# Moving the first five parts of a head's scan later in the product stream of the next head (HGRN2, odd heads)

## The chip, the cores and the metric

The kernel runs on one core of a Trainium2 chip. The metric is the device time of one execution in microseconds (us), as the median of several runs. The engines are TensorE (PE in the profile; its weight loads are PEld), VectorE (DVE), ScalarE (ACT), GpSimd (POOL) and SyncE (SP, which issues most of the transfers). Each engine works through its own instructions in the order in which they were written, and waits on the others through semaphores.

## The reference, cut to what matters

One step of a two-layer decoder over 512 prompt tokens and 64 sample tokens (8 sequences of 8), width 1024, all in float32. Layer 0 mixes tokens with HGRN2, a gated linear recurrence with 8 heads of width 128; layer 1 uses an S5 state-space model. The change touches layer 0's mixer alone:

```python
q, fz, v, g = jnp.split(x @ w_in, 4, axis=-1)
f = lbf + (1.0 - lbf) * sigmoid(fz)
qh = heads(silu(q) * HG_QK_SCALE); kh = heads(1.0 - f)
# per head: S_t = diag(f_t) S_{t-1} + k_t v_t^T,  o_t = S_t^T q_t
o, s = hgrn2_chunk_scan(qh, kh, heads(v), heads(log(f)), s0)
o = rms_norm(o, gnorm_w) * silu(heads(g))
return o @ w_out, s
```

The prompt starts from a zero state, the sample sequences from given states; the new states of both are outputs.

## The kernel before, in words

**Products.** A float32 product is made of three matmuls of split operands (`mm3`, lines 299 to 301: high by high, high by low, low by high). "A product" below means one such triple, over one of the 8 slices of the width. The projections of a head are written by the generator `proj(h)`, which gives back control after every product. The weights of f, q and g take 16 products each: 8 for the first 320 tokens, into one PSUM bank, and 8 for the other 256, into a second one. So an odd head has 48 products, numbered 0 to 47 (0 to 7 with 320 columns, 8 to 15 with 256, and so on). An even head first has 40 products more, the value projection V for itself and the head after it.

**What is written between the products.** After each product the loop at the end of `hgrn()` writes one step of the oldest of the `sides` (`decay`, `factors`, `queries`: the elementwise work of a head on ACT, DVE and POOL), and then the steps of `scan(h-1)`, the recurrence of the head before, that the table `SCAN_AT` lists for this number. `SCAN_AT[0]` is for even heads and `SCAN_AT[1]` for odd ones. Head 0 has no scan to carry, so the odd row serves four heads, 1, 3, 5 and 7, with the scans of heads 0, 2, 4 and 6. Nothing else sets the order: what is written first stands first in its engine's queue.

**The sides around the place.** `factors(h-1)` runs in the last third of `proj(h-1)` and ends with the decayed keys K2 and the factors QL and E2. `queries(h-1)` counts nine empty steps (`QWAIT`) and so acts at products 9 to 12 of the next head: at 9, ACT copies both PSUM banks of g, loads the Silu table, applies Silu to a 128 by 1152 tile and loads the log/exp table again; at 10 to 12, DVE writes QH, the three pieces of QL, and Q2.

**The scan's 16 steps.** Step 1 transposes K2 on PE (line 661), copies the result into kT on ACT and has POOL mask the values into vm. Step 2 transposes the sample part (line 668) and copies it. Step 3 multiplies kT by V (line 674), copies the first of four states to S on ACT and adds up the other three on DVE, and has SP send the last one out. Step 4 makes the sample state updates on PE (line 688, one bank from the ring `tr`, one from the ring `mm`), and DVE adds the first four of them to So; step 5 adds the other four. Steps 6 to 9 are the attention blocks within a chunk of 128 tokens (lines 704 and 709: KH by QH, and KL by QL); step 6 also has SP send So out. Steps 10 to 16 make the outputs.

**Banks.** The ring `tr` has two banks, taken in turn by steps 1, 2, 3, 4 (its first bank) and 6. So step 6 takes the bank that step 3 had, and its first matmul may run only when ACT and DVE have read that bank; step 3 takes the bank of step 1, and step 4 that of step 2. The ring `mm` of four banks serves the products and step 4. In the trace, names lose their last digits: K is K2, Q is Q2, S and So are as written, and many DVE and ACT operations carry the line of a helper (L200, L203, L206, L197).

Of the kernel before, what the change touches and what calls it, by code (L numbers as in the profile page):

```python
# [62 lines left out]
SY = ((6, 8), (8, 8), (6, 10), (6, 2))  # L63
QY = ((3, 3), (2, 5), (1, 3), (1, 2))
SPLIT_S5 = 14
SCAN_AT = ((2, 4, 10, 16, 20, 26, 30, 34, 38, 42, 46, 50, 54, 60, 68, 74), (2, 4, 6, 9, 12, 15, 17, 19, 21, 23, 26, 33, 34, 36, 41, 45))
QWAIT = 9
SIDE = 1
OCT = 2
# [73 lines left out]
def hybrid_decoder_kernel(ctx: ExitStack, tc: tile.TileContext, a: dict):  # L143
# [329 lines left out]
    def hgrn():  # L473
# [52 lines left out]
        def proj(h):  # L526
            if h % 2 == 0:
                p = take(16)
                V[h // 2] = hp.tile([128, 5, 256], FP32, tag="V", name="V", bufs=2)
                for i in range(5):  # L530
                    c = slice(i * 128, i * 128 + 128) if i < 4 else slice(T - 128, T)
                    ps = mm_bank()
                    for k in range(KD):
                        hi, lo = w_ap(p + 2 * k, 256)
                        mm3(ps[:, :256], xhih[:, k, c], xloh[:, k, c], hi, lo, k == 0, k == KD - 1)
                        yield
                    copy(V[h // 2][:, i, :], ps[:, :256])
                free_to(p + 16)
            d = hd[h] = {}

            yield from two_units(take(8))
            sides.append(decay(h, d, hd["ps"]))

            yield from two_units(take(8))
            sides.append(factors(d, hd["ps"]))
            yield from two_units(take(8))
            sides.append(queries(h, d, hd["ps"]))
# [217 lines left out]
        for h in range(H):  # L765
            at = SCAN_AT[h % 2]
            for n, _ in enumerate(proj(h)):
# [1128 lines left out]
```

## Time and profile before

| | us |
|---|---|
| median of 3 runs | 1589.3 |
| lowest, highest | 1586.47, 1589.44 |
| profiled execution, its own time | 1589.6 |
| its span, first to last instruction | 1587.8 |
| PE busy in the span | 1514.9 (95%) |
| DVE busy | 947.1 (60%) |
| ACT busy | 687.9 (43%) |
| mean granted PE clock | 0.983 |

The profile gives, for each row of a timeline, the start in us from the span's start, the length of the row in us, the engine, the line, the operation with its output and inputs, and in brackets how long the engine had been idle before and who released it. Matmuls overlap, so the time of a product is read from one start to the next, not from its length. Rows of windows give the stretch, its length, the busy time of PE, PEld, DVE, ACT and POOL with the number of instructions, the granted PE clock (1.00 is full speed), the DMA share and GB/s.

### The profile page before, as it was taken

How to read it: one execution, taken by the hardware profiler on the slowest of the kernel's cores; microseconds unless marked ns; L12 is line 12 of the kernel's file. 1: busy time of each engine (PE TensorE's matmuls, PEld its weight loads, DVE VectorE, ACT ScalarE, POOL GpSimd, SP SyncE). 2: the span in 40 equal slices, each digit the busy share in tenths (PEclk: the TensorE clock that was granted, in tenths of full speed). 3: DMA queues.
4: the chain of work that ended last, by engine and by line, in shares of the span. 5: the costliest groups of instructions: out<-in, count | busy, mean ns of one | idle time of the engine just before them, and what ended most of it. 6: DMA issues, size and time to landing. Idle time of an engine off the chain costs nothing. (4 is left out here: it accounts for less than half of the span.)

```text
span 1587.8 us, 30040 instructions
## 1 busy us (share of the span) xinstructions
PE 1514.9 (95%) x12550; PEld 1467.1 (92%) x12550; DVE 947.1 (60%) x1711; ACT 687.9 (43%) x1152; POOL 342.9 (22%) x447
## 2 busy tenths in 40 slices
PE   8899999899999999999999947999999999999998
PEld 7898989788999999999989947899999999999997
DVE  4848484868547778953486699457433233334685
ACT  5546464746532223123278524436432222123375
POOL 1303030302003768860022332302000000000111
PEclk9999999999999999999999978999999999999999
DMA  5223131232224877663214986432222222223121
GB/s 185 95 69 101 63 109 64 100 115 80 68 70 145 216 185 216 195 182 108 98 54 170 233 209 179 101 107 80 67 80 93 80 81 93 81 80 120 31 78 60
DMA packets 97255, 180.32 MB, mean 114 GB/s; under 512 B 41888, under 2 KB 56912, under 8 KB 96864
## 3 DMA queue, kind: packets, MB, share of 16 engines
q1 hardware_dynamic: 88144, 151.92, 31.3%
q0 software_dynamic: 8976, 26.49, 6.2%
q8 instruction: 98, 1.61, 0.4%
q14 instruction: 37, 0.30, 0.1%
HBM read 151.08 MB, written 27.30 MB: 112 GB/s over the span
## 5 line engine op out<-in xcount | busy, mean ns | idle before, releaser
L299 PE MATMUL mm<-xh,whi 128*128 128x288 f32 x2048 | 609.7, 298 | 9.5 <-ACT xh L200 6.5
L300 PE MATMUL mm<-xl,whi 128*128 128x288 f32 x2048 | 608.9, 297 | 5.0 <-POOL xl L203 3.5
L301 PE MATMUL mm<-xh,wlo 128*128 128x288 f32 x2048 | 606.6, 296 | 1.3 <-DVE wlo L203 1.3
L299 PEld LDWEIGHTS mm<-xh,whi 128*128 128x128 f32 x2048 | 387.8, 189 | 15.9 <-ACT xh L200 7.6
L300 PEld LDWEIGHTS mm<-xl,whi 128*128 128x128 f32 x2048 | 387.9, 189 | 8.4 <-POOL xl L203 5.0
L301 PEld LDWEIGHTS mm<-xh,wlo 128*128 128x128 f32 x2048 | 387.8, 189 | 1.5 <-DVE wlo L203 1.5
L200 ACT ACTIVATE whi<-wraw 128x1024 fp32r<-128x1024 f32 x208 | 218.7, 1053 | 250.1 <-DMA wraw<-in_w_dram 117.2
L203 DVE TENSOR_TENSOR wlo<-wraw,whi 128x1024 fp32r<-128x1024 f32 x200 | 247.1, 1252 | 33.2 <-ACT whi L200 32.8
L299 PE MATMUL mm<-hhi,whi 128*128 128x288 f32 x704 | 209.3, 297 | 0.0
L301 PE MATMUL mm<-hhi,wlo 128*128 128x288 f32 x704 | 207.5, 295 | 0.0
L300 PE MATMUL mm<-hlo,whi 128*128 128x288 f32 x704 | 207.2, 294 | 0.0
L203 DVE TENSOR_TENSOR fs<-fs,mm 128x288 f32<-128x288 f32 x88 | 39.9, 454 | 254.5 <-PE mm L301 241.4
L203 POOL TENSOR_TENSOR ln_s<-ln_s,xf 128x288 f32<-128x288 f32 x24 | 24.3, 1012 | 570.9 <-DVE xf L203 451.2
L299 PEld LDWEIGHTS mm<-hhi,whi 128*128 128x128 f32 x704 | 132.1, 188 | 1.7 <-issue 1.4
L300 PEld LDWEIGHTS mm<-hlo,whi 128*128 128x128 f32 x704 | 132.1, 188 | 0.3
L301 PEld LDWEIGHTS mm<-hhi,wlo 128*128 128x128 f32 x704 | 132.0, 188 | 0.0
L299 PE MATMUL mm<-xhi,whi 128*128 128x320 f32 (+1 forms) x384 | 121.5, 316 | 0.0
L300 PE MATMUL mm<-xlo,whi 128*128 128x320 f32 (+1 forms) x384 | 113.3, 295 | 0.0
L301 PE MATMUL mm<-xhi,wlo 128*128 128x320 f32 (+1 forms) x384 | 113.2, 295 | 0.0
L200 ACT ACTIVATE hhi<-fs 128x288 fp32r<-128x288 f32 x88 | 38.8, 441 | 152.1 <-DVE fs L203 152.1
L197 ACT ACTIVATE fs<-mm,eps 128x288 f32<-128x288 f32 x88 | 44.1, 502 | 131.0 <-PE mm L301 130.9
L299 PEld LDWEIGHTS mm<-xhi,whi 128*128 128x128 f32 x384 | 72.7, 189 | 6.9 <-issue 4.4
(318 smaller groups left out, 2273.9 us busy)
## 6 DMA issues: line engine op xcount, KB each, us to landing
wraw<-in_w_dram SPq DMA_DIRECT2D x198, 512.0 KB
wraw<-in_w_dram POOLq DMA_DIRECT2D x10, 512.0 KB, 7.1
S<-in_s_dram SPq DMA_DIRECT2D x8, 512.0 KB
out_hgs_dram<-So SPq DMA_DIRECT2D x8, 512.0 KB
wr<-wt_scratch SPq DMA_DIRECT2D x16, 256.0 KB
bT<-in_s5bt_dram SPq DMA_DIRECT2D x16, 256.0 KB
cl_scratch<-cl POOLq DMA_DIRECT2D x16, 256.0 KB, 6.1
zw_scratch<-zw POOLq DMA_DIRECT2D x16, 256.0 KB, 6.5
```

The costliest lines, as they stand in the source:

```text
L197: nc.scalar.activation(out, in_, func, bias=ZERO if bias is None else bias, scale=scale)
L200: nc.scalar.activation(out, in_, ACT.Copy)
L203: (eng or nc.vector).tensor_tensor(out, x, y, op=op)
L299: nc.tensor.matmul(out, whi, rhi, start=start, stop=False)
L300: nc.tensor.matmul(out, whi, rlo, start=False, stop=False)
L301: nc.tensor.matmul(out, wlo, rhi, start=False, stop=stop)
```

## The change

In the odd row of `SCAN_AT`, the first five of the sixteen numbers become larger, and the other eleven stay. Step 1 is written after product 7 instead of 2, step 2 after 8 instead of 4, step 3 after 12 instead of 6, step 4 after 13 instead of 9, step 5 after 14 instead of 12. Step 6 stays after product 15. No instruction is added or removed.

```diff
-SCAN_AT = ((2, 4, 10, ...), (2, 4, 6, 9, 12, 15, 17, 19, 21, 23, 26, 33, 34, 36, 41, 45))
+SCAN_AT = ((2, 4, 10, ...), (7, 8, 12, 13, 14, 15, 17, 19, 21, 23, 26, 33, 34, 36, 41, 45))
```

The queues of SP and POOL are in the same order as before. On DVE, in each of the four heads, the state sums of steps 3 and 4 stood ahead of the queries' three operations; this piece of the difference is the first head's (467 to 469 are head 0's K2, E2 and S0, 604 and 624 its Q2).

```order
 L203 TENSOR_TENSOR wlo<-wraw,whi 128x1024 x2
+L206 SCALAR_TENSOR_TENSOR QH<-qg,QH 128x576
+L206 SCALAR_TENSOR_TENSOR QL<-qg,QL 128x256 x3
+L206 SCALAR_TENSOR_TENSOR Q_604<-qg,E_468 128x576
 L206 SCALAR_TENSOR_TENSOR S<-S,E_468,tr 128x128 x3
 L206 SCALAR_TENSOR_TENSOR So<-S_469,E_468,tr 128x128 x4
-L206 SCALAR_TENSOR_TENSOR QH<-qg,QH 128x576
-L206 SCALAR_TENSOR_TENSOR QL<-qg,QL 128x256 x3
-L206 SCALAR_TENSOR_TENSOR Q_624<-qg,E_468 128x576
 L206 SCALAR_TENSOR_TENSOR So<-S_469,E_468,mm 128x128 x4
```

QH, QL and Q2 now stand ahead of the sums S and the first half of So, which read the two `tr` banks.

On ACT, the copy of the first state stood ahead of the queries' copies, their two table loads and the Silu.

```order
-L200 ACTIVATE S<-tr 128x128
 L200 ACTIVATE qg<-mm 128x320
 L200 ACTIVATE qg<-mm 128x256
 L197 ACT_TABLE_LOAD
 L197 ACTIVATE qg<-qg,eps 128x1152
 L641 ACT_TABLE_LOAD
+L200 ACTIVATE S<-tr 128x128
 L200 ACTIVATE whi<-wraw 128x1024
```

It now stands behind the second table load.

On PE, these are the rows from the sample updates of step 4 to the attention block of step 6, before the change (the six products between the second and the third row left out; tr_603 and tr_640 are uses of the two `tr` banks), with what each waits for.

```order
L688 MATMUL tr_603<-vm_557,kT_550 128x512 [waits Activation_49,Pool_49]
L688 MATMUL mm_604<-vm_557,kT_550 128x512 [waits Activation_49]
...
L704 MATMUL tr_640<-QH_464,KH_463 128x128 [waits DVE_49]
L709 MATMUL tr_640<-QL_466,KL_465 16x16 [waits DVE_49]
L709 MATMUL tr_640<-QL_466,KL_465 16x16 x3
L709 MATMUL tr_640<-QL_466,KL_465 32x32 [waits DVE_49]
```

And with the change, from step 3 on (the products between the steps left out: one between steps 3 and 4, two before step 6).

```order
L674 MATMUL tr_606<-V_163,kT_568 128x128 [waits Activation_49]
L674 MATMUL tr_606<-V_163,kT_568 128x128 x3
...
L688 MATMUL tr_621<-vm_575,kT_568 128x512 [waits Activation_49,Pool_49]
L688 MATMUL mm_622<-vm_575,kT_568 128x512 [waits Activation_49]
...
L704 MATMUL tr_640<-QH_464,KH_463 128x128 [waits DVE_49,Activation_49]
L709 MATMUL tr_640<-QL_466,KL_465 16x16 x4
```

Between step 3 and step 6 nine products stood before and three stand now, and the first matmul of step 6 now waits for ACT as well as for DVE.

More of the change, by code (lines that the diff above doesn't have):

```diff
@@ L65 @@
 SPLIT_S5 = 14
-SCAN_AT = ((2, 4, 10, 16, 20, 26, 30, 34, 38, 42, 46, 50, 54, 60, 68, 74), (2, 4, 6, 9, 12, 15, 17, 19, 21, 23, 26, 33, 34, 36, 41, 45))
+SCAN_AT = ((2, 4, 10, 16, 20, 26, 30, 34, 38, 42, 46, 50, 54, 60, 68, 74), (7, 8, 12, 13, 14, 15, 17, 19, 21, 23, 26, 33, 34, 36, 41, 45))
 QWAIT = 9
```

## Prediction

> **What bounds the kernel now.** I read the page's busy times first, then a row of windows over layer 0's heads, then the list of waits.
>
> ```profile
> PE 1514.9 (95%) x12550; PEld 1467.1 (92%) x12550; DVE 947.1 (60%) x1711; ACT 687.9 (43%) x1152; POOL 342.9 (22%) x447
> 0.00:323.64 323.64, 304.06 (x2531) 278.65 (x2531) 208.09 (x352) 189.33 (x308) 56.04 (x60) 0.98 0.28 97
> PE tr L661 <- DVE K L203: 9.3, 4, 3.9
> ```
>
> PE sets the time. Time is won only where PE stops waiting or runs at a higher clock, and lost where it begins to wait. In the heads PE is idle for 19.6 us of 323.64, and 9.3 us of that are four waits of step 1 (line 661) for K2, one in each odd head: just where the change begins. Everything later in the kernel needs the heads' output, and PE is the busy engine behind them, so I carry each gain or loss in the heads to the end unchanged.
>
> The timeline shows the place in head 5, on PE, then ACT, then DVE (head 3 shows the same wait).
>
> ```profile
> 129.00 0.66 PE L661 MATMUL tr<-cst,K 128*128 128x128 f32 x4 [1.79 <-DVE K L203]
> ...
> 205.83 0.66 PE L661 MATMUL tr<-cst,K 128*128 128x128 f32 x4 [1.80 <-DVE K L203]
> 206.24 0.40 PE L299 MATMUL mm<-xhi,whi 128*128 128x320 f32 x1
> 206.77 0.31 PE L299 MATMUL mm<-xhi,whi 128*128 128x320 f32 x1
> 207.21 0.27 PE L668 MATMUL tr<-cst,K 128*128 128x128 f32 x1
> 208.21 1.05 PE L674 MATMUL tr<-V,kT 128*128 128x128 f32 x8
> 209.01 0.39 PE L299 MATMUL mm<-xhi,whi 128*128 128x320 f32 x1
> 210.34 0.69 PE L688 MATMUL tr<-vm,kT 32*128 32x512 f32 x1
> 211.39 0.38 PE L299 MATMUL mm<-xhi,whi 128*128 128x256 f32 x1
> 211.85 0.28 PE L299 MATMUL mm<-xhi,whi 128*128 128x256 f32 x1
> 212.21 0.28 PE L299 MATMUL mm<-xhi,whi 128*128 128x256 f32 x1
> 213.62 0.46 PE L704 MATMUL tr<-QH,KH 128*128 128x128 f32 x2
> 214.86 0.42 PE L299 MATMUL mm<-xhi,whi 128*128 128x320 f32 x1
> 215.84 0.38 PE L704 MATMUL tr<-QH,KH 128*128 128x128 f32 x2
> 216.65 0.42 PE L299 MATMUL mm<-xhi,whi 128*128 128x320 f32 x1
> ```
>
> ```profile
> 207.40 0.87 ACT L200 ACTIVATE kT<-tr 128x512 f32<-128x512 f32 x2
> 209.47 0.71 ACT L200 ACTIVATE qg<-mm 128x320 f32<-128x320 f32 x2
> 211.49 1.26 ACT L197 ACTIVATE qg<-qg,eps 128x1152 f32<-128x1152 f32 x1
> 212.76 1.28 ACT L641 ACT_TABLE_LOAD   x1
> ...
> 204.72 1.06 DVE L203 TENSOR_TENSOR K<-K,k 128x576 f32<-128x576 f32 x1 [0.84 <-ACT K L197]
> 209.60 1.11 DVE L206 SCALAR_TENSOR_TENSOR S<-S,E,tr 128x128 f32<-128x128 f32 x3 [0.71 <-ACT S L200]
> 212.78 0.76 DVE L206 SCALAR_TENSOR_TENSOR QH<-qg,QH 128x576 f32<-128x576 f32 x1 [0.16 <-ACT qg L197]
> 215.13 1.12 DVE L206 SCALAR_TENSOR_TENSOR So<-S,E,mm 128x128 f32<-128x128 f32 x4
> ```
>
> From starts: a product takes 0.44 us with 320 columns (206.77 to 207.21) and 0.36 with 256 (211.85 to 212.21), or 0.46 just behind other matmuls (211.39 to 211.85). The four transposes of step 1 take 0.41, step 3 takes 0.80 (208.21 to 209.01), step 4 takes 1.05. The attention block takes 1.24 the first time (213.62 to 214.86), when it still waits for pieces of QL, and 0.81 the next (215.84 to 216.65).
>
> **The change part by part.** *Step 1 behind five more products.* In head 5 PE is free at 205.83 - 1.80 = 204.03. Five products of 0.44 take it to 206.23, and K2 is done at 204.72 + 1.06 = 205.78: the wait is gone. It comes to 1.8 us in head 3 as well, and the sum of 9.3 leaves 1.8 for head 7. In the first of the four, head 1, the wait is longer, and these are its rows:
>
> ```profile
> 50.44 1.02 PE L661 MATMUL tr<-cst,K 128*128 128x128 f32 x4 [3.89 <-DVE K L203]
> 54.37 1.05 PE L674 MATMUL tr<-V,kT 128*128 128x128 f32 x8
> 59.79 0.47 PE L704 MATMUL tr<-QH,KH 128*128 128x128 f32 x2
> 61.03 0.42 PE L299 MATMUL mm<-xhi,whi 128*128 128x320 f32 x1
> 51.77 0.58 ACT L200 ACTIVATE kT<-tr 128x512 f32<-128x512 f32 x1
> 58.95 0.76 DVE L206 SCALAR_TENSOR_TENSOR QH<-qg,QH 128x576 f32<-128x576 f32 x1 [0.16 <-ACT qg L197]
> 52.73 1.91 POOL L664 TENSOR_TENSOR vm<-V,cst 64x512 f32<-64x512 f32 x1
> ```
>
> There 1.69 of 3.89 us stay (46.55 + 2.20 = 48.75, to 50.44).
>
> *Steps 2 to 5 close up, and step 6 stays.* With no wait PE comes to step 6 in head 5 at: 206.23 + 0.41 (step 1) + 0.46 (product 8) + 0.03 (step 2, hidden beside the product) + 0.46 + 3 x 0.36 (products 9 to 12) + 0.80 (step 3) + 0.46 (product 13) + 1.05 (step 4) + 0.46 + 0.36 (products 14, 15) = 211.80, against 213.62 before. If nothing else waited, that would be the 1.8 us, won.
>
> *What is late next: the bank of step 6.* Step 6 takes the `tr` bank that step 3 wrote. Before, ACT and DVE had read it by 209.60 + 1.11 = 210.71, long before 213.62. Now both reads stand behind the queries. ACT's copies of kT still wait for an unmoved weight conversion, so they end at 207.40 + 0.87 = 208.27 as before. The queries' copies follow at 208.17 (rows on ACT overlap by 0.1), 1.30 earlier than before, since the copy of S is out of the way. From there to QH it took 212.78 - 209.47 = 3.31, so QH starts at 211.48. QH, QL and Q2 took 215.13 - 212.78 = 2.35, so the sums S run from 213.83 to 214.94. ACT's copy of S, behind the second table load, is done at about 211.48 + 1.28 + 0.3 = 213.1: DVE decides. With 0.05 for the release (205.78 to 205.83), line 704 starts at 214.99. PE has come at 211.80: **a new wait of 3.2 us** in place of one of 1.8. QL is complete by then, so the block takes 0.81 and the next product starts at 215.80, against 214.86: **0.94 slower**. Heads 3 and 7 have the same wait and, by their rows, the same spacing.
>
> In head 1: kT to 52.64, copies 52.54, QH 55.85, S 58.20 to 59.31, line 704 at 59.36, next product 60.17, against 61.03: **0.86 faster**. PE comes there at 56.57: 50.44 + 5.57 and 0.56 more, as step 4, due at 54.13, needs POOL's vm, which ends at 52.73 + 1.91 = 54.64. So PE waits 2.8 us.
>
> Sum of the waits: 3 x 0.94 - 0.86 = +2.0 us. So's other half and the next head's decay come behind S on DVE, about as late as PE itself (215.13 becomes 215.97); no new wait follows from it. Behind the waiting line 704 on PE stand only products, whose reader, the next head's decay on ACT, has its inputs already. SP's last state (line 680) now waits for S until 214.94, with only So's transfer behind it in the queue until the next head's weights: nothing.
>
> *The clock.* These are rows of windows along the 3.41 us grid on which the granted clock (third number from the right) changes, the stretch ahead of a change and those after it.
>
> ```profile
> 50.58:53.99 3.41, 3.41 (x15) 3.37 (x15) 3.15 (x2) 2.04 (x4) 3.33 (x3) 0.50 0.26 66
> ...
> 125.67:129.09 3.42, 1.62 (x12) 1.36 (x12) 2.58 (x4) 2.01 (x5) 3.34 (x5) 1.00 0.15 61
> 129.09:132.50 3.41, 3.41 (x27) 3.40 (x28) 2.97 (x2) 2.36 (x5) 0.76 (x1) 1.00 0.13 28
> ...
> 313.40:316.82 3.42, 1.40 (x9) 1.16 (x10) 3.42 (x15) 3.37 (x13) 0.00 (x0) 1.00 0.05 18
> 316.82:320.23 3.41, 3.41 (x11) 1.68 (x10) 2.31 (x9) 3.36 (x8) 0.00 (x0) 0.50 0.08 24
> 320.23:323.64 3.41, 3.41 (x16) 3.31 (x14) 3.41 (x9) 3.25 (x4) 0.00 (x0) 0.50 0.00 0
> ```
>
> A stretch with PE busy 1.40 us (idle 2.0) was followed by half clock; one with 1.62 (idle 1.8, head 3's present wait) was not. So the old waits of 1.8 us are too short to cost clock, and a new one costs it when 2.0 us or more fall into one stretch. An idle of 3.2 misses only if its part in the first stretch is between 1.2 and 2.0: 0.8 of 3.41 positions, so it hits in 77%; 2.8 us hits in 65%. That makes 3 x 0.77 + 0.65 = 3.0 drops. The price: in head 1, after 3.89 us, step 1 to step 3 took 54.37 - 50.44 = 3.93 us, in head 5 at full clock 2.38: 1.55. It is the upper end. At the lower, up to 1.2 us of the wait reach into the slow stretch: 1.55 x 2.2 / 3.41 = 1.0. I take 1.2, since attention blocks with small matmuls lie in it. Sum: **+3.6 us**. The present drop of head 1 needs no term of its own, since its row for line 704 contains it.
>
> The Trainium skill (TensorE: Matmul & The Clock Gate, HAM oscillation — how this bites in real kernels) states the rule as no idle gaps of PE over about 3.4 us. By that rule the new waits would cost no clock, and the sum would stay at +2.0. The stretch of 313.40, busy for 1.40 us in part and still followed by 0.50, speaks against the rule as worded; the row decides.
>
> Together 2.0 + 3.6 = +5.6 on the profiled execution's 1589.6 us: 1595.2. That execution lies 0.3 above the median of 1589.3, so the forecast is **1595 us**.
>
> **The rivals.**
>
> *The waits without the clock drops.* +2.0 us, 1591.3. For it: the limit of 2.0 us rests on one stretch in this list, and the grid may lie kindly. Against it: four chances, each at 65% or more.
>
> *The bank isn't what step 6 waits for, or is read in time; QH decides, as now.* Then line 704 starts at 211.48 + 0.76 + 0.05 = 212.29 in head 5, and with the block's 1.24 the next product at 213.53: 1.33 faster; in head 1 at 56.66, and 57.90: 3.13 faster. Together 3 x 1.33 + 3.13 = 7.1: 1582.5. For it: the sums S are only 1.11 us, and PE's old waits do vanish. It decides once S ends 0.9 us earlier than I work out (line 704 by 214.05, break-even). Against it: in the new order line 704 waits for ACT too, which only the copy of S explains, and DVE's queue has S behind Q2.
>
> *The drops last for two stretches.* For it: after 313.40 the clock stayed at 0.50 for two stretches running, although PE counted as busy in both. Three more stretches at 1.5: +4.5, 1599.5. Against it: in head 1 one stretch was all.
>
> *The change doesn't remove the old wait.* K2 would have to be over 0.4 us later than 205.78 in head 5, and nothing ahead of it on ACT or DVE moves. No chance of its own.
>
> **How the numbers follow.** Forecast 62%, no drops 17%, two stretches 10%, QH decides 11%. The likeliest case alone spans two drops at 1.0 to four at 1.55, 1593.3 to 1597.5. For 8 in 10 the range takes in the case without drops and most of the doubled one: 1590.5 to 1599. This kernel's measurement can tell about 0.2%, 3.2 us, from no change: no drops (+2.0) counts as the same, 17%; forecast and doubled drops as slower, 72%; QH as faster, 11%.
>
> **What would show it.** In the changed profile: no wait of line 661 for K in heads 3, 5 and 7, and under 2 us in head 1; line 704 waiting for DVE S (or ACT S) for about 3 us four times, 12.4 us in all in place of 9.3; S starting about 2.4 us behind QH; half clock in the stretch after two to four of these waits, and none at head 1's step 1. Wrong would be the bank if line 704 follows QH by 0.1 us; the clock term if the waits are there and the clock stays at 1.00; the assumption that all carries through if layer 0's heads end later by 5 us and the whole kernel doesn't.

## The result, and the profile after

| | us |
|---|---|
| the kernel before, median beside it | 1589.2 |
| the changed kernel, median | 1599.69 |
| its lowest and highest | 1595.72, 1601.78 |
| ratio to before, with its 95% interval | 1.0067, 1.0048 to 1.0085 |

The changed kernel is 10.5 us slower. The direction is the one forecast; the forecast of 1595 had 5.8 us of it, and the measured time lies 0.7 us above the range.

The waits of PE in the changed kernel (profiled span 1600.0 us), the two rows that the change made or shortened:

```profile
PE tr L704 <- DVE S L206: 13.2, 4, 3.5
PE tr L661 <- DVE K L203: 1.1, 1, 1.1
```

Step 1 waits for K2 in head 1 alone, 1.1 us instead of 9.3 in four heads. Step 6 waits for S four times, 13.2 us in all. Head 5 on PE, then on DVE and ACT:

```profile
211.01 0.60 PE L661 MATMUL tr<-cst,K 128*128 128x128 f32 x4
220.16 0.63 PE L704 MATMUL tr<-QH,KH 128*128 128x128 f32 x2 [3.46 <-DVE S L206]
228.93 0.64 PE L719 MATMUL tr<-S,Q 128*32 128x128 f32 x16
...
216.56 0.76 DVE L206 SCALAR_TENSOR_TENSOR QH<-qg,QH 128x576 f32<-128x576 f32 x1 [2.71 <-ACT qg L197]
218.91 1.11 DVE L206 SCALAR_TENSOR_TENSOR S<-S,E,tr 128x128 f32<-128x128 f32 x3
...
217.84 0.28 ACT L200 ACTIVATE S<-tr 128x128 f32<-128x128 f32 x1
```

S starts 2.35 us behind QH and ends at 220.02, line 704 starts at 220.16; ACT's copy of S was done 2 us earlier. The next view is the windows along the clock's grid at the four places (stretch, its length, busy time of PE, PEld, DVE, ACT, POOL, granted clock, DMA share, GB/s): for each head the stretch with the wait and those that follow.

```profile
56.48:59.89 3.41, 0.80 (x16) 0.67 (x16) 3.34 (x11) 2.28 (x5) 0.00 (x0) 1.00 0.02 7
59.89:63.31 3.42, 3.42 (x25) 2.92 (x25) 1.68 (x7) 1.64 (x2) 0.00 (x0) 0.50 0.47 174
63.31:66.72 3.41, 3.41 (x24) 3.01 (x25) 3.38 (x4) 0.77 (x1) 0.00 (x0) 0.50 0.00 0
134.99:138.40 3.41, 1.50 (x10) 0.77 (x6) 2.04 (x5) 3.37 (x5) 0.00 (x0) 1.00 0.50 171
138.40:141.81 3.41, 1.85 (x18) 1.48 (x18) 3.34 (x13) 1.24 (x3) 0.00 (x0) 0.50 0.09 24
141.81:145.23 3.42, 3.42 (x25) 3.01 (x25) 1.64 (x4) 2.03 (x3) 0.00 (x0) 0.50 0.38 153
216.91:220.32 3.41, 0.16 (x1) 0.19 (x2) 3.34 (x10) 2.92 (x5) 0.00 (x0) 1.00 0.14 55
220.32:223.73 3.41, 3.41 (x24) 2.82 (x23) 2.13 (x8) 1.21 (x2) 0.00 (x0) 0.50 0.32 118
223.73:227.15 3.42, 3.42 (x44) 3.05 (x44) 2.92 (x4) 1.21 (x2) 0.00 (x0) 1.00 0.15 60
295.41:298.83 3.42, 0.79 (x6) 0.58 (x5) 2.75 (x7) 3.39 (x5) 0.00 (x0) 1.00 0.34 122
298.83:302.24 3.41, 2.60 (x20) 2.22 (x21) 3.07 (x11) 0.77 (x3) 0.00 (x0) 0.50 0.07 19
302.24:305.65 3.41, 3.41 (x25) 3.01 (x25) 1.94 (x2) 2.15 (x3) 0.00 (x0) 0.50 0.38 154
```

All four waits are followed by half clock, three of them for two stretches: seven slow stretches, against one in these heads before (head 1's step 1). Followed mark by mark through the two timelines, the changed kernel is 11.1 us behind when the last scan begins (its line 661 at 323.3, before at 312.1), 11.9 us behind at that scan's step 10 (line 719 at 342.5, before at 330.6), and 12.1 us behind at the last product. So nearly all of it comes from the heads, and nothing later gives it back. In the last scan, which adds 0.8 us, two other things differ: step 6 waits 2.6 us for QH, before 0.2, and one stretch is slow (from 336.4), before two (316.82 to 323.64).

### The profile page after: what moved, and what is told of

It reads as the page before. It is cut to its first block, busy times and chain, and to the rows that moved or that the text cites. A ratio compares the mean times of both kernels' runs of the same rounds, so it can differ in the third digit from the quotient of the medians.

```text
span 1600.0 us, 30044 instructions
## 1 busy us (share of the span) xinstructions
PE 1519.6 (95%) x12550; PEld 1472.0 (92%) x12550; DVE 942.0 (59%) x1711; ACT 688.2 (43%) x1152; POOL 341.7 (21%) x447
## 5 line engine op out<-in xcount | busy, mean ns | idle before, releaser
L203 POOL TENSOR_TENSOR ln_s<-ln_s,xf 128x288 f32<-128x288 f32 x24 | 24.2, 1010 | 573.0 <-DVE xf L203 451.2
```

The costliest lines, as they stand in the source:

```text
L203: (eng or nc.vector).tensor_tensor(out, x, y, op=op)
```

## The experiments

The theory after the result: the bank of step 6 makes a wait as worked out (some 2 to 3 us in all over the waits that it replaces), and the rest, 8 us, is the clock. All kernels below are the changed kernel with the edit shown, unless another is named; each ratio is to the kernel before, run beside it.

### Filling the wait with idle-time matmuls

```diff
             Q2 = d["Q2"]
+            if h % 2 == 0:
+                fill = bank("os", 1)
+                for _ in range(12):
+                    nc.tensor.matmul(fill, xhih[:, 0, 0:128], xhih[:, 1, 0:512], start=True, stop=True)
             ps = tr_bank()
```

> The changed kernel with 12 idle-time matmuls (128 by 512 columns, into the bank os, which is free there) written ahead of step 6 in the four odd heads; they are extra work whose result nobody reads. At about 0.22 us each they fill 2.6 us of the new waits of 2.8 to 3.5 us and leave the waits' ends where they are. If the doubled loss is the clock (theory): no half-clock stretch at the four places, and only the waits' own +2.4 us over the kernel before is left (each head's line 704 at the offsets that the changed kernel's trace has without its slow stretches), about 1591.5. If the waits themselves or something downstream cost the 10.5 us (rival): 1599 to 1600 as in the changed kernel.

Measured: 1591.67 us, ratio 1.0017 (1.0006 to 1.0027). In this kernel the lines behind the edit are higher by four: step 6 is line 708, the row of the filling carries L704, and line 719 is L723. Head 5 on PE, the waits, and the windows behind three of the four waits:

```profile
211.62 2.22 PE L704 MATMUL os<-xhi 128*128 128x512 f32 x9
214.54 0.46 PE L708 MATMUL tr<-QH,KH 128*128 128x128 f32 x2 [0.69 <-DVE S L206]
221.87 0.65 PE L723 MATMUL tr<-S,Q 128*32 128x128 f32 x16
...
PE tr L708 <- DVE S L206: 2.1, 3, 0.7
...
60.46:63.88 3.42, 3.42 (x45) 2.96 (x44) 1.64 (x3) 2.24 (x3) 0.00 (x0) 1.00 0.38 153
138.97:142.38 3.41, 3.41 (x44) 2.99 (x44) 1.84 (x2) 2.25 (x3) 0.00 (x0) 1.00 0.38 154
217.48:220.89 3.41, 3.41 (x45) 2.95 (x44) 2.28 (x3) 1.81 (x3) 0.00 (x0) 1.00 0.36 141
```

Step 6 still starts when S is done, but PE has been busy until 0.7 us before, and the clock stays at 1.00. Nothing else was changed, so the 8.0 us between 1599.69 and 1591.67 are the price of the clock (7.9 us by the two ratios, whose intervals leave some 3 us either way), and about 2.7 us (0.17%) that of the waits. The same shows in the stretch from line 704 to line 719, which holds no wait: 7.33 us here (214.54 to 221.87), 8.77 us in the changed kernel's head 5 (220.16 to 228.93), a difference of 1.44 us for one slow stretch. The other heads of the changed kernel give 2.80 (head 1), 2.14 (head 3) and 2.47 (head 7) for two stretches each, 8.9 us in all in the profiled execution.

### The changed kernel once more

> The changed kernel once more, for a second look at the clock. Theory: line 704 waits for S at the same 2.8 and 3.5 us to within 0.1, since the order makes the waits; but which of the four places lose one slow stretch and which two differs, since it depends on where a wait falls in the grid. Where the wait reaches into the first slow stretch, a second follows; where it doesn't, mostly not. Rival: the same four lengths (6.8, 6.8, 3.4, 6.8) again, fixed by the instructions.

Measured: 1599.13 us, ratio 1.0057 (1.0037 to 1.0077). The waits for S are 13.2 us in all again, 3.5 the longest. The windows behind them (the slow stretches of the four heads, and the one after in head 1):

```profile
58.81:62.23 3.42, 3.42 (x35) 2.95 (x36) 1.83 (x7) 1.52 (x2) 0.00 (x0) 0.50 0.42 157
62.23:65.64 3.41, 3.41 (x44) 2.99 (x44) 3.23 (x4) 0.89 (x2) 0.00 (x0) 1.00 0.05 20
137.32:140.73 3.41, 2.95 (x22) 2.57 (x23) 2.75 (x10) 0.77 (x2) 0.00 (x0) 0.50 0.14 44
140.73:144.15 3.42, 3.42 (x25) 3.02 (x25) 2.30 (x3) 1.79 (x3) 0.00 (x0) 0.50 0.33 133
219.24:222.65 3.41, 3.41 (x25) 2.89 (x25) 1.67 (x7) 1.64 (x2) 0.00 (x0) 0.50 0.44 171
297.75:301.16 3.41, 3.25 (x23) 2.87 (x24) 2.46 (x10) 0.89 (x2) 0.00 (x0) 0.50 0.21 76
301.16:304.57 3.41, 3.41 (x25) 2.91 (x24) 2.59 (x4) 1.53 (x2) 0.00 (x0) 0.50 0.24 97
```

Again all four places lose clock, now one, two, one and two stretches. Head 1 has one where it had two before. Two follow where PE is not busy throughout the first slow stretch (2.95 and 3.25 us of 3.41), that is, where the wait reaches into it. That fits heads 3, 5 and 7 of the first profile too; head 1 there (3.42 busy, and still two) it doesn't explain.

### Only products behind the wait

```diff
-(7, 8, 12, 13, 14, 15, 17, 19, 21, 23, 26, 33, ...)
+(7, 8, 12, 13, 14, 15, 24, 26, 28, 30, 31, 33, ...)
```

> The changed kernel with step 6 at its place (so with the same wait) but steps 7 to 11 later, so that eight products and no attention blocks follow the first block. Theory A (the slow clock lasts for a second stretch because the attention blocks keep PE too little busy in the first): single slow stretches at all four places, 3 to 4 us under the changed kernel, 1596. Theory B (it lasts because of the rest of the wait that reaches into the stretch, or of where the stretch lies): doubled stretches as in the changed kernel, 1599 to 1600.

Measured: 1600.22 us, ratio 1.0073 (1.0058 to 1.0089). The first slow stretch of each head, and the second of head 1:

```profile
56.51:59.93 3.42, 1.73 (x17) 1.36 (x18) 3.35 (x12) 1.37 (x3) 0.00 (x0) 0.50 0.09 24
59.93:63.34 3.41, 3.41 (x14) 3.41 (x14) 1.63 (x4) 1.90 (x3) 0.00 (x0) 0.50 0.38 154
138.43:141.85 3.42, 3.37 (x23) 2.99 (x24) 2.35 (x9) 1.01 (x2) 0.00 (x0) 0.50 0.27 97
220.35:223.76 3.41, 3.41 (x15) 3.41 (x14) 1.67 (x7) 1.64 (x2) 0.00 (x0) 0.50 0.44 168
298.86:302.27 3.41, 3.22 (x23) 2.85 (x24) 2.48 (x10) 0.87 (x1) 0.00 (x0) 0.50 0.20 74
```

Two, two, one and two stretches, and no time won: the attention blocks are not what keeps the clock low. One stretch follows only in head 5, where PE is busy from the first to the last moment.

### Step 3 in another bank

```diff
-            ps = tr_bank()
+            ps = tr_bank() if h % 2 else bank("o", 1)
             for j in range(4):
                 nc.tensor.matmul(ps[:, j * 128:j * 128 + 128], kT[:, j, :], Vh[:, j, :], start=True, stop=True)
```

> The changed kernel with step 3's products in the bank o instead of the ring tr in the four odd heads, so that step 6 needn't wait for S. If the bank is what step 6 waits for (theory): line 704 follows QH by 0.1 us, PE waits there under 1 us, no half clock at the four places, and the time is that worked out for the rival QH decides, 7 us under the kernel before, 1582. If not the bank but DVE's or ACT's order as such holds PE (rival): line 704 still waits for S, 1599.

Measured: 1592.97 us, ratio 1.0021 (1.001 to 1.0031). The waits of PE, DVE in head 5, and the stretch with the wait of line 735 in head 5 with the one behind it:

```profile
PE tr L704 <- DVE QH L206: 2.4, 4, 0.8
PE os L735 <- DVE ats L727: 6.2, 4, 1.6
...
223.28 3.84 DVE L580 TENSOR_TENSOR_SCAN b<-seg,L 128x576 f32<-128x576 bf16 x3
227.05 1.19 DVE L203 TENSOR_TENSOR wlo<-wraw,whi 128x1024 fp32r<-128x1024 f32 x1
228.17 0.71 DVE L713 COPY_PREDICATED att<-msk,tr 128x512 f32<-128x512 uint32 x1
228.91 0.23 DVE L727 COPY_PREDICATED ats<-msk,tr 64x64 f32<-64x64 uint32 x1
...
225.84:229.25 3.41, 1.86 (x15) 1.60 (x13) 3.35 (x6) 1.62 (x3) 0.00 (x0) 1.00 0.00 0
229.25:232.67 3.42, 3.42 (x14) 3.30 (x15) 3.42 (x7) 2.27 (x3) 1.73 (x1) 0.50 0.80 307
```

The bank was the cause: line 704 now follows QH, and up to there each of heads 3, 5 and 7 is 1.2 us faster than before. But the time isn't 1582. PE now reaches step 13 (line 735) 1.6 us before the masked copy that it needs, which stands on DVE behind the decay's scans of the next head and a weight split; three of the four such waits (heads 1, 3 and 5) are followed by a slow stretch, and the gain is more than gone.

### Steps 6 to 11 later

```diff
-(7, 8, 12, 13, 14, 15, 17, 19, 21, 23, 26, 33, ...)
+(7, 8, 12, 13, 14, 23, 24, 25, 26, 27, 28, 33, ...)
```

> The changed kernel with steps 6 to 11 also later (after products 23 to 28 instead of 15, 17, 19, 21, 23, 26), so that eight more products (3.5 us) stand between step 5 and step 6. Theory: S is read by the time PE comes to step 6, PE waits under 0.3 us there, no half clock, and the whole of the old waits is won: heads 3, 5, 7 1.8 + 0.4 us each, head 1 3.9 - 1.1 of its wait, 1.5 of its slow stretch and 0.4, less 0.5 for POOL's vm: 10 to 11 us under the kernel before, 1579. Rival (moving the scan later delays the next head's K2 or its own outputs): no faster than the kernel before, with a new wait in the even heads.

Measured: 1594.82 us, ratio 1.0038 (1.0024 to 1.0052). No wait of line 704 in the odd heads, but:

```profile
PE os L735 <- DVE ats L727: 10.2, 4, 2.7
```

The same wall, hit harder, since PE comes to it earlier. The time of 1579 was wrong for the same reason.

### Steps 12 to 16 later as well

In the kernel with bank o, and in the one with late steps 6 to 11:

```diff
-(..., 26, 33, 34, 36, 41, 45)
+(..., 26, 37, 39, 41, 45, 47)
```

```diff
-(..., 28, 33, 34, 36, 41, 45)
+(..., 28, 39, 42, 43, 46, 47)
```

> The kernel with step 3 in the bank o, and steps 12 to 16 later (after products 37, 39, 41, 45, 47 instead of 33, 34, 36, 41, 45). Theory: what undid that kernel's gain was step 13 on PE (line 735), which waited 1.6 us per odd head for the masked copies that stand behind the decay's scans on DVE, and the half clock behind each of these waits. Five products more (1.8 us) cover it: no wait of line 735, no half clock in the odd heads, 7 us under the kernel before, 1582. Rival: DVE's lag passes on to the next head's K2 or to the outputs, so that a new wait of the same size stands at line 661 in the even heads or at line 752: 1588 to 1593.

> The kernel with steps 6 to 11 after products 23 to 28, and steps 12 to 16 later too (39, 42, 43, 46, 47). Same theory: its line 735 waited 2.6 us per odd head; eight products more cover it, and the 10 us that it had won up to there stay won, 1579, or 1580 to 1581 if the outputs of head 6 come late for what follows the last head. Rival: the lag passes on, 1589 to 1595.

Measured: 1592.42 us, ratio 1.0024 (1.0013 to 1.0036), and 1598.86 us, ratio 1.0057 (1.0039 to 1.0075). Line 735 no longer waits; the first row is of the first kernel, the second of the second:

```profile
PE tr L752 <- ACT sq L197: 9.6, 4, 2.4
```

```profile
PE tr L752 <- ACT sq L197: 12.2, 4, 3.2
```

The rival was right: the lag passes on, to the squares of step 14, which now stand on ACT behind the next head's factors. The two kernels differ in the clock. In the profile of the first, each of the four waits of 2.4 us is split by the grid over two stretches, the emptiest of which is this one, and none is followed by half clock:

```profile
309.19:312.61 3.42, 1.90 (x17) 1.69 (x15) 2.57 (x3) 2.73 (x7) 3.34 (x5) 1.00 0.07 26
```

So this kernel loses its gain to the waits alone, while each of the four waits of the second, 2.7 to 3.2 us long, costs clock as well. Moving the scan within the head chooses the place at which PE waits for DVE and ACT. Neither is full there: from step 1 of head 5 to the next step 1, 30.4 us in the kernel before, DVE is busy for 24.2 us and ACT for 21.5. That the chain in which the two wait for each other is about as long as PE's work is argued and not measured; the kernel with less work for DVE, further down, agrees with it.

### The queries four products later

```diff
-            for _ in range(QWAIT):
+            for _ in range(QWAIT if h % 2 else 13):
```

> The changed kernel with the queries of the four heads acting four products later (13 to 16), so that S again stands ahead of QH on DVE and ACT. If the place of S behind the queries makes the wait (theory): line 704 no longer waits for S but for QH, which comes after Silu at 0.4 us behind the kernel before; the wait is 2.2 us instead of 3.2, and the time lies between the two kernels, 1592 to 1597. If the wait for S has another cause (rival): line 704 still released by S after 3 us or more, 1599 to 1600.

Measured: 1600.72 us, ratio 1.0071 (1.0055 to 1.0088). S stands ahead of QH again, and the waits of PE are:

```profile
PE tr L704 <- DVE QH L206: 7.5, 5, 1.6
PE tr L709 <- DVE QL L206: 3.2, 4, 0.9
```

The wait for S is gone, so its place behind the queries made it. But the late queries make two others, of QH and of QL right after it, which together are long enough to cost clock at all four places, and the time is that of the changed kernel. The time expected for this run was wrong.

### Less work for DVE

In the kernel with bank o (steps 12 to 16 at their old places), the one weight split per odd head that stands between the scans and the masked copies is given to POOL:

```diff
                 for _ in range(at.count(n) if g else 0):
                     step(g)
+                st["lo"] = nc.gpsimd if h % 2 and 15 <= n < 23 else nc.vector
```

> The kernel with step 3 in the bank o (steps 12 to 16 at their old places), and the one low weight split per odd head that stands on DVE between the decay's scans and the masked copies given to POOL, which has nothing to do there. Theory: DVE's chain in an odd head, not PE, is what the later scan runs into; 1.2 us less on it takes line 735's wait from 1.6 us to about 0.4, too short to cost clock, and the 7 us that step 6 won stay: 1582 to 1584. Rival: the next thing on DVE or ACT (the squares before line 752, the next head's K2) takes up the lag, or POOL's work slows DVE: 1588 to 1593.

Measured: 1585.55 us, ratio 0.9978 (0.9967 to 0.9988): faster than the kernel before, by 2.9 us beside it, and so the best of all here. Its waits in the odd heads:

```profile
PE tr L704 <- DVE QH L206: 2.6, 4, 0.8
PE os L735 <- DVE ats L727: 1.8, 4, 0.5
PE tr L752 <- ACT sq L197: 1.3, 4, 0.3
```

No single wait is over 0.8 us, and no slow stretch is left in the odd heads. The 2.9 us are less than half of the 7 expected: of the 1.2 us that step 6 gains in each of heads 3, 5 and 7, the way from line 719 to line 752, with the short waits of lines 735 and 752, takes back about 1 us, and what stays is mostly head 1. The same edit in the kernel before (old table, step 3 in the ring):

> The kernel before with only the low weight split of the odd heads given to POOL (old table, step 3 in the ring tr). Theory: with the old table PE comes to line 735 about 0.5 us after the masked copies are ready, so 1.2 us less on DVE are worth nothing by themselves: the four waits of line 661 and the slow stretch of head 1 stay, 1588 to 1589. Rival (it was the split alone that won the 3 us): 1585 to 1586.

Measured: 1592.97 us, ratio 1.003 (1.0018 to 1.0042): slower. So the split alone wins nothing. Why it loses was not expected; the windows of head 5, at its old wait of line 661, and DVE a little later show:

```profile
202.71:206.12 3.41, 1.57 (x12) 1.30 (x11) 2.57 (x3) 2.71 (x6) 3.33 (x4) 1.00 0.01 4
206.12:209.53 3.41, 3.41 (x16) 3.37 (x15) 2.27 (x2) 1.62 (x3) 0.05 (x1) 0.50 0.35 112
...
217.21 1.78 DVE L568 TENSOR_SCALAR e<-e 128x576 f32<-128x576 f32 x1
```

The wait of 1.8 us, which cost no clock in the kernel before, is now followed by half clock in heads 5 and 7, with PE busy for 1.57 us of the stretch ahead instead of 1.62 or more. The row of DVE, 0.46 us long before, takes 1.78 while POOL runs the split. Whether the one leads to the other was not tried.

## Why the prediction was right on the direction and wrong on the size

*Step 1 behind five more products*: right. No wait for K2 in heads 3, 5 and 7, and 1.1 us in head 1 (1.69 forecast).

*The bank of step 6*: right. S 2.35 us behind QH, line 704 released by S, 13.2 us of waits (12.4 forecast). The kernel with another bank for step 3 shows that it was the bank. The term of the waits was +2.0 us; the kernel with the waits filled measures about 2.7.

*The clock*: the mechanism was right, and its term is the step that failed: +3.6 us were forecast, and about 8 measured (1599.69 less 1591.67), 8.9 in the profiled execution. Two figures in it were too small. Three drops were counted on, from a limit of 2.0 us of idle time in one stretch; all four waits cost clock in both profiles of the changed kernel, and in the kernel with only products behind the wait. By the prediction's own chances four of four comes in 30% of cases, so a part of this may be luck; but the limit was too high as well, since idle time of 1.84 us (1.57 busy) was enough in the kernel with the split on POOL, and 1.55 us (1.86 busy) in the one with bank o. The larger error is the price: a drop was taken as one stretch at 1.2 us, which would have made 4.8 us of four drops; one stretch measures 1.4, and five of eight drops lasted two, 2.1 to 2.8 us. "The drops last for two stretches" stood among the rivals with 10% and 1599.5; it is what happened, in three of four heads.

*The rule of the Trainium skill* (TensorE: Matmul & The Clock Gate, HAM oscillation — how this bites in real kernels), no idle gaps over about 3.4 us, would have given 1591.3 with the waits as worked out, and 1591.67 is what the kernel takes when they are filled. Three of the four waits came out at 3.5 us, about the rule's figure, and so say little on it; the wait of 2.8 us in head 1, which cost clock in both profiles, and those of 1.6 us in the kernel with bank o decide against the rule as worded.

*The rival "QH decides"* (1582.5) was wrong in its bank, and its time was wrong as well: with the bank out of the way the kernel takes 1592.97, because the prediction had looked for the next late thing only as far as step 6. It said that no new wait follows behind S; that held in the changed kernel, where PE itself is late, and not once PE is early.

*That a loss carries through to the end*: right; 11.9 us at the last head's scan and 12.1 at the last product.

## What to carry to other kernels

Before moving work past a wait, list what each moved instruction is put behind on every engine and which buffer's release hangs on it: here one PSUM bank, read late, made a wait of 3.5 us out of one of 1.8. Price a wait of PE with what it does to the clock: on this kernel one slow stretch cost 1.4 us, and two 2.1 to 2.8. Every wait of 2.7 us or more at these places was followed by at least one; waits of 1.6 to 2.4 us went both ways, and the four of 2.4 us that the grid split cost none. Filling such a wait with matmuls whose result nobody reads got that price back. And when DVE and ACT follow close behind PE, moving PE's wait wins little: with the bank out of the way the kernel took 1592.97 us, and only with less work on DVE as well 1585.55.

## What the runs showed of the hardware that was not expected

- Half clock followed idle times well below the stretch of 3.41 us, and the busy time of PE in the stretch does not settle it alone. It followed PE busy for 1.57 and 1.58 us in the kernel with the split on POOL, for 1.86 us three times in the kernel with bank o, and for 2.40 us in head 7 of the kernel with the later queries. It did not follow 1.62 and 1.63 us in the kernel before, nor 1.90 us in the one with bank o and later steps 12 to 16. What else counts was not tried.
- In the odd heads a slow stretch in which PE was not busy throughout was followed by a second one in each of the cases shown above (1.85, 2.60, 2.95, 3.25, 1.73, 3.37, 3.22 us busy). Where it was busy throughout, the clock came back after one, but not in head 1 of the changed kernel's first profile; and full clock followed 3.34 us busy in the kernel with late steps 6 to 11 and 3.04 in head 1 of the kernel before with the split on POOL. What decides there stays open.
- In the kernel before with the split on POOL, the DVE row of line 568, 0.46 us otherwise, took 1.78 us in each of the odd heads, beside a POOL weight split of 2.38 us that had begun 0.9 us earlier; in head 5 the two end 0.3 us apart:

```profile
216.30 2.38 POOL L203 TENSOR_TENSOR wlo<-wraw,whi 128x1024 fp32r<-128x1024 f32 x1 [10.13 <-ACT whi L200]
```

The Trainium skill (SBUF — State Buffer, Who interferes with whom) gives DVE and POOL one port pair as an exclusive lock: a DVE operation in a mode that takes both of its ports, as `tensor_scalar` can, and a POOL operation wait for each other's whole instruction, the later for the earlier. Whether the row ran in such a mode no profile shows. The rows agree with the lock, as does the kernel with bank o and the split on POOL: there the split ends 0.4 us before the row of line 568 begins, and the row takes 0.46 us.
